# Output projection of six heads by seven half-size products, with sums of y kept in DRAM

## The chip, the cores and the metric

One core of a Trainium2 chip runs the whole step. TensorE multiplies, VectorE, ScalarE and GpSimd work on the tiles in SBUF, and DMA queues (issued by SyncE, called SP, and by GpSimd) move data to and from DRAM. The metric is the device time of one execution in microseconds. The kernel before takes 1073.28 us (median of 3 runs, 1072.37 to 1074.58).

## The reference

One step of a decoder trunk of two layers on 1024 new tokens and 8 x 4 tokens of running sequences, 1056 in all. Layer 1 is a gated linear recurrence; layer 2, where the change lies, has eight heads of 128 (HGRN2):

```python
xn = _rmsnorm(x, g_norm)
u = (xn @ w_in).astype(jnp.float32)
q, f, iv, gate = jnp.split(u, 4, axis=-1)
...                                   # per head: gated recurrence over the tokens -> o
o = o * lax.rsqrt(jnp.mean(o * o, axis=-1, keepdims=True) + EPS) * o_gain...
y = (o.reshape(Bsz, T, INNER_B) * jax.nn.silu(gate)).astype(x.dtype)
return x + y @ w_out, ...
```

The output is the RMS norm of that sum, and the new states. `y @ w_out` (1056 x 1024 by 1024 x 1024) is the output projection.

## The kernel before, in words

Activations lie transposed: a row of a head or of a model block is a tile of 128 x 1056, tokens along the free axis; NCH = 3 chunks of CH = 352, two halves of HT = 528, four quarters of QT = 264. Every float32 product is made of three fast matmuls (`mm3`, L241 to L243): operand and weight are each split into a high part (a cast, by ScalarE) and a low part (value minus high part), and high x high, low x high, high x low are added up in PSUM. "Splitting" a tile means making those two parts. `subtract(e, ...)` makes the low part by a real subtraction on engine e (L328); `low` (L312 to L315) makes it by a ScalarE copy of -x and a DMA from GpSimd's queue that adds.

Instructions are collected in a flow per engine (`pe`, `act`, `dve`, `pool`, `dma` add one each, with an estimated duration, what it reads and writes, and a priority), and a planner orders each engine's list by these before the program is built. `inherit` says whose place in memory a new tile takes. The order of each engine is fixed then; at run time the engines wait for one another by semaphores.

Layer 2's input projection of heads 1 to 7 is made in pairs of row blocks by `seven(h, a, b, order, at)`: a 2 x 2 block product by seven half-size products (the Strassen-Winograd form), each product 2 halves of 12 matmuls of 264 columns. Its order strings name the products 1 to 7; a letter b is a place where one of the four bursts of the recurrence is put between the products. burst1 to burst4 of head h hold the decay levels of head h beside the outputs of head h - 1; burst4(h) ends with `gated(h - 1)`, which writes that head's y to the row `SG[h - 1]` (two rows, by turns). In the bursts GpSimd makes `vb` (L1198) and `rst` (L1302). The decay products of a head (L1048) start in the row `Gc`, whose first one is of level 1 and 528 wide; the scalings that use them are L1039.

For heads 0 to 5 `gated` also stores y to a DRAM tensor `yd`. The output projection then has two parts. The early part takes K1 = 5 heads: 24 products of 15 matmuls (one of 8 model blocks, one of 3 chunks of 352 columns), with pieces of y read back from `yd` and split by ScalarE and then VectorE or GpSimd (`splits`, `yparts`). VectorE adds each product to x in place (L1635; `x2` lists the rows where x lies). The last six bursts (burst3 of head 7 to burst4 of "head 8", which only ends head 7) are put between its products (`SPOTS1`). The late part (`late`) takes the other three heads: 24 products of 9 matmuls, of 424, 376 and 256 columns (`OUT`), added to x by VectorE (L1732), followed by the squares, their sums and the scaling of the final norm (L1702 to L1743), which run beside it.

Of the kernel before, what the change touches and what calls it, by code (L numbers as in the profile page):

```python
# [25 lines left out]
K1 = 5  # L26
NMM = 3
HC = 1
FQ0, FQ, GV = "1267b4b35", "12b675b43", "126b74b53"
SPOTS, SPOTS0, SPOTS1 = (6, 9, 0, 2), (2, 5, -1, -1), (1, 5, 9, 13, 17, 20)  # L30
# [9 lines left out]
CH = 352  # L40
# [169 lines left out]
def tile_trunk(ctx: ExitStack, tc: tile.TileContext, xT, prm, hc, w0, wg, wo0, w1, wo1, s_in,  # L210
# [85 lines left out]
    with ExitStack() as l0:  # L296
# [603 lines left out]
        yd = [nc.dram_tensor(f"yd_{h}", (128, TOK), F32, kind="Internal").ap() for h in range(H - 2)]  # L900
# [32 lines left out]
    with ExitStack() as l1:  # L933
# [8 lines left out]
        ls2 = [fixed(f"land{i}", [128, CH], F32, p1) for i in range(1)]  # L942
# [402 lines left out]
        def burst4(h):  # L1345
            s = next(hg)
            run(together([*([gated(h - 1, *s)] if h else []), *([levels3264(h, *s), values(h, (0,))] if h < H else [])]))

# [53 lines left out]
        def seven(h, a, b, order, at=()):  # L1402
# [166 lines left out]
        yh, yl = (list(o[:4]) for o in (xh, xl))  # L1569
        flat = {k: o.rearrange("p x j t -> p (x j t)") for k, o in TB.items()}  # L1570
        for k in ((2, 0), (3, 0), (4, 0), (4, 1)):
            yh.append(flat[k][:, :TOK])
            yl.append(flat[k][:, TOK:])
        for k in range(H):
            if k < 4:
                olds = [("x", 1, k, x) for x in range(2)] + [("T", 1, i, k, x) for i in range(2) for x in range(2)]
            else:
                n, i = ((2, 0), (3, 0), (4, 0), (4, 1))[k - 4]
                olds = [("T", n, i, j, x) for j in range(4) for x in range(2)]
            for o in ("yh", "yl"):  # L1580
                for c in range(NCH):
                    inherit((o, k, c), olds)

        def splits(k, cs, eng):

            for c in cs:
                if k < H - 2:
                    x, xk = next(land)
                    dma(x, yd[k][:, chunk(c)], (("yd", k),), (xk,), 3)
                    xk = (xk,)  # L1590
                else:
                    x, xk = SG[k][:, chunk(c)], ykeys(k % 2, c * CH, CH)
# [4 lines left out]
        def yparts(c):  # L1597
            return [(yh[k][:, chunk(c)], yl[k][:, chunk(c)], (("yh", k, c), ("yl", k, c))) for k in range(K1)]

        own = []  # L1600
        for i, o in enumerate(ks):
            key = ("k", i, 1)
            inherit(key, [("s", j) for j in range(6) if j * QT < (i + 1) * CH and (j + 1) * QT > i * CH])
            own.append((o[0], key))
        own.sort(key=lambda o: max(fl.readers.get(o[1]) or [0]))
        land2 = [(o, ("land", i)) for i, o in enumerate(ls2)]
        land = chain(land2, own[:3], [(t[:, :CH], k) for t, k in rawq if k[0] == "W"], cycle(own))
        for c in range(NCH):
            for k in range(K1):
                splits(k, (c,), V if k % 3 < 2 else G)  # L1610
        splits(5, range(NCH), G)


        side = cycle(banks8[NMM:4])
        raws = cycle([r for r in rawq if r[1][0] == "raw"])
        x2 = [Gs, R[:, 3], R[:, 2], R[:, 1], Bs, B2, VT, Gc]
        old = [GK, [("W", i) for i in range(5 - NRAW)], eight("A", 0), eight("A1"), eight("B"), eight("B2"), [("VT", i) for i in range(4)],
               [("Gc", l) for l in (1, 2, 4, 8, 16, 32)]]
        last = {s: f for s, f in zip(SPOTS1, (lambda: burst3(H - 1), lambda: burst4(H - 1), lambda: burst1(H), lambda: burst2(H),
                                            lambda: burst3(H), lambda: burst4(H)))}  # L1620
        ws2 = {}
        for n, (m, c) in enumerate([(m, c) for c in range(NCH) for m in range(2)] + [(m, c) for m in range(2, KD) for c in range(NCH)]):
            if m not in ws2:
                at_ = None
                if m < 2:
                    at_ = [(flat[m + 2, 1][:, i * 640:i * 640 + 640], ("wt", m, i)) for i in range(2)]
                    for _, k in at_:
                        inherit(k, [("T", m + 2, 1, j, x) for j in range(4) for x in range(2)])
                ws2[m] = weights(wo1[m][:, :128 * K1], 128 * K1, at=at_)
                for k in ykeys(Y2 + m, 0, TOK):  # L1630
                    inherit(k, old[m])
            x, xk = x2[m][:, chunk(c)], ykeys(Y2 + m, c * CH, CH)
            dma(x, x1d[m][:, chunk(c)], (), xk, 3)
            ps, pk = product(ws2[m], yparts(c), 8 if m > 1 else 1)
            dve(CH, lambda x=x, ps=ps: V.tensor_tensor(x, ps[:, :CH], x, op=ALU.add), (pk, *xk), xk, 0)  # L1635
            if n in last:
                last[n]()
                if n == SPOTS1[1]:
                    splits(6, range(NCH), V)
                if n == SPOTS1[5]:  # L1640
                    splits(7, range(NCH), V)

# [3 lines left out]
        for m in range(KD):  # L1646
            row = (xh, xl)[m // 4][4 + m % 4]
            hi, lo, hk, lk = row[:, :nl], row[:, nl:2 * nl], ("late", m, 0), ("late", m, 1)
            for k in (hk, lk):
                inherit(k, [("x", p, m % 4, x) for p in (2, 3) for x in range(2)])  # L1650
            raw, rk = next(raws)
            dma(raw[:, :nl], wo1[m][:, 128 * K1:], (), (rk,), 1, nl / 2)
            act(nl, lambda hi=hi, raw=raw: S.copy(hi, raw[:, :nl]), (rk,), (hk,), 1)
            pool(nl, lambda hi=hi, lo=lo, raw=raw: G.tensor_tensor(lo, raw[:, :nl], hi.bitcast(F32), op=ALU.subtract), (rk, hk), (lk,), 1)
            late.append((hi, lo, (hk, lk)))
# [56 lines left out]
        for a, n in OUT:  # L1712
# [4 lines left out]
            for m in range(KD):  # L1717
# [12 lines left out]
                pe(9 * n / 2200, emit, (*wk, *((o, K1 + k, c) for o in ("xh", "xl") for k in range(K2) for c in cs)), (pk,))  # L1730
# [90 lines left out]
```

## Time and profile before

| what | value |
|---|---|
| median of 3 runs | 1073.28 us (1072.37 to 1074.58) |
| the profiled execution | 1074.84 us, its span 1073.1 us |
| mean granted TensorE clock | 0.994 |
| busy: PE, DVE, ACT, POOL | 1050.9, 745.6, 663.7, 504.5 us |
| the early part of the output projection | 942.65 to 1023.43 us |
| the late part | 1023.43 to 1061.02 us, then the tail to 1073.1 |

Times inside the profile are microseconds from the span's start. PE is TensorE's matmuls, PEld its weight loads, DVE is VectorE, ACT ScalarE, POOL GpSimd and SP the queue of DMAs. Matmuls are pipelined, so a matmul's own length is longer than its pace; the pace is read from a stretch of many.

### The profile page before, as it was taken

The page shows a single profiled execution, that of the slowest core. Times are in us where ns is not written, and L with a number is a line of the kernel's source. Part 1 is how long each engine was busy: PE and PEld are TensorE (multiplying, and loading weights), DVE is VectorE, ACT ScalarE, POOL GpSimd, SP SyncE. Part 2 cuts the span into 40 slices and gives each one's busy share as a digit, 9 for nine tenths or more (in the row PEclk, how much of TensorE's full clock was granted, in tenths as well). Part 3 has the DMA queues.
Part 4 walks back from the last instruction along what each step waited for, and adds up shares of the span by engine and source line. Part 5 has one row for each costly group of instructions (what it writes and reads, how often), then busy time and mean ns, then how long its engine had stood idle before and what let it go on. Part 6 is the DMA issues. An engine that isn't in the chain of part 4 may idle for free.

```text
span 1073.1 us, 25672 instructions
## 1 busy us (share of the span) xinstructions
PE 1050.9 (98%) x10020; PEld 1023.3 (95%) x10020; DVE 745.6 (69%) x1481; ACT 663.7 (62%) x1493; POOL 504.5 (47%) x536
## 2 busy tenths in 40 slices
PE   9999999999999999999989999999999999999997
PEld 9999999999999999999989998989999999989996
DVE  7999996887987787274887556556565475674446
ACT  6578656867765964243467685858586767652323
POOL 3425353354543547455454454455455464541544
PEclk9999999999999999999989999999999999999999
DMA  9111112124832785373675564746465657555204
GB/s 302 60 28 43 56 48 72 58 60 127 270 104 67 217 258 168 108 242 121 188 200 110 130 140 100 178 93 156 89 151 112 155 112 169 140 161 166 84 1 162
DMA packets 92490, 139.59 MB, mean 130 GB/s; under 512 B 11344, under 2 KB 60496, under 8 KB 92368
## 3 DMA queue, kind: packets, MB, share of 16 engines
q1 hardware_dynamic: 75952, 109.49, 31.8%
q0 software_dynamic: 14112, 25.70, 14.3%
q10 hardware_dynamic: 2304, 2.77, 0.8%
q8 instruction: 78, 1.28, 0.5%
q14 instruction: 44, 0.36, 0.1%
HBM read 77.54 MB, written 29.81 MB: 100 GB/s over the span
## 4 chain that ended last, share of the span: by engine, by line
PE 86%; DVE 9%; DMA 3%; issue 1%; ACT 1%; POOL 0%; POOLq 0%; ACTq 0%; SPq 0%; DVEq 0%
PE mm L241 24%; PE mm L242 24%; PE mm L243 23%; PE hg L1057 2%; PE hg L1166 2%; DMA a<-xn 1%; PE hg L1274 1%; PE hg L572 1%; DVE R L1039 1%; PE hg L1276 1%; PE hg L241 1%; PE hg L242 1%; PE hg L243 1%; PE hg L1220 1%; DVE a L1240 1%
## 5 line engine op out<-in xcount | busy, mean ns | idle before, releaser
L241 PE MATMUL mm<-xh,whi 128*128 128x352 f32 (+1 forms) x1111 | 346.6, 312 | 5.7 <-DVE sg L1510 5.7
L242 PE MATMUL mm<-xl,whi 128*128 128x352 f32 (+1 forms) x1111 | 340.7, 307 | 0.0
L243 PE MATMUL mm<-xh,wlo 128*128 128x352 f32 (+1 forms) x1111 | 340.6, 307 | 0.0
L241 PEld LDWEIGHTS mm<-xh,whi 128*128 128x128 f32 x1111 | 209.0, 188 | 8.3 <-DVE sg L1510 6.8
L242 PEld LDWEIGHTS mm<-xl,whi 128*128 128x128 f32 x1111 | 209.3, 188 | 1.5
L243 PEld LDWEIGHTS mm<-xh,wlo 128*128 128x128 f32 x1111 | 209.1, 188 | 0.0
L328 POOL TENSOR_TENSOR wlo<-wraw,whi 128x512 fp32r<-128x512 f32 (+1 forms) x72 | 96.3, 1347 | 105.7 <-ACT whi L383 97.2
L241 PE MATMUL mm<-t,whi 128*128 128x264 f32 (+1 forms) x354 | 104.0, 294 | 0.0
L243 PE MATMUL mm<-t,wlo 128*128 128x264 f32 (+1 forms) x354 | 101.8, 288 | 2.0 <-DMA wlo<-wraw 2.0
L242 PE MATMUL mm<-t,whi 128*128 128x264 f32 (+1 forms) x354 | 101.9, 288 | 0.0
L504 DVE SCALAR_TENSOR_TENSOR k<-xb,prm_sb,k 128x352 f32<-128x352 f32 (+2 forms) x144 | 90.0, 636 | 11.0 <-ACT k L501 6.3
L315 POOL DMA_DIRECT2D wlo<-wraw x59 | 51.6, 888 | 65.6 <-ACT wlo L314 46.6
L1510 DVE TENSOR_TENSOR k<-mm,k 128x264 f32<-128x264 f32 x72 | 30.7, 430 | 62.2 <-PE mm L243 59.4
L243 PEld LDWEIGHTS mm<-t,wlo 128*128 128x128 f32 x354 | 67.2, 190 | 2.3 <-DMA wlo<-wraw 2.3
L241 PEld LDWEIGHTS mm<-t,whi 128*128 128x128 f32 x354 | 67.5, 191 | 0.5 <-ACT k L1487 0.2
L242 PEld LDWEIGHTS mm<-t,whi 128*128 128x128 f32 x354 | 67.5, 191 | 0.0
L587 POOL TENSOR_TENSOR k<-X 128x352 f32<-128x352 f32 x36 | 42.8, 1198 | 47.8 <-DVE R L588 38.6
L383 ACT CAST whi<-wraw 128x512 fp32r<-128x512 f32 (+2 forms) x75 | 41.3, 569 | 31.3 <-PE mm L242 19.8
L315 POOL DMA_DIRECT2D wlo<-R x36 | 33.5, 929 | 49.7 <-ACT wlo L314 48.2
L241 PE MATMUL mm<-yh,whi 128*128 128x352 f32 x153 | 49.9, 326 | 0.0
L243 PE MATMUL mm<-yh,wlo 128*128 128x352 f32 x153 | 49.4, 323 | 0.0
L242 PE MATMUL mm<-yl,whi 128*128 128x352 f32 x153 | 49.4, 323 | 0.0
(422 smaller groups left out, 2742.1 us busy)
## 6 DMA issues: line engine op xcount, KB each, us to landing
wraw<-in_w_dram SPq DMA_DIRECT2D x88, 256.0 KB, 3.1
wlo<-wraw POOLq DMA_DIRECT2D x59, 256.0 KB, 4.1
wlo<-R POOLq DMA_DIRECT2D x36, 256.0 KB, 4.0
wraw<-in_wo_dram SPq DMA_DIRECT2D x34, 192.0 KB, 2.5
si<-in_s_in_dram SPq DMA_DIRECT2D x8, 512.0 KB, 4.5
R<-in_w_dram SPq DMA_DIRECT2D x16, 256.0 KB, 3.8
out_ss_out_dram<-si SPq DMA_DIRECT2D x8, 512.0 KB, 2.6
sg<-x1b SPq DMA_DIRECT2D x21, 176.0 KB, 3.1
```

The costliest lines, as they stand in the source:

```text
L241: T.matmul(out, wh, xh, start=first, stop=False, skip_group_check=chained)
L242: T.matmul(out, wh, xl, start=False, stop=False, skip_group_check=chained)
L243: T.matmul(out, wl, xh, start=False, stop=last, skip_group_check=chained)
L315: fl.add("POOL", 0.93, lambda: G.dma_start(dst.bitcast(F32), src, accum_op=ALU.add), (*r, *w), w, prio, n / 2)
L328: emit = lambda: e.tensor_tensor(b, x, a.bitcast(F32), op=ALU.subtract)
L383: act(m, lambda hi=hi, raw=raw, m=m: S.copy(hi[:, :m], raw[:, :m]), rk, (hk,), prio)
L504: dve(u, lambda src=src, dst=dst, sh=sh, k=k: V.scalar_tensor_tensor(dst, sh(src, k), pc("cw", 12 * k + m), dst, op0=ALU.mult, op1=ALU.add ...
L572: fl.add("PE", 0.62, lambda ps=ps, i=i, c=c: T.matmul(ps[:96, :CH], gs[:, i, :], ST[:96, chunk(c)], start=True, stop=True), (("gs",), *((" ...
L587: pool(CH, lambda x=x, a=a, b=b: G.tensor_tensor(x, a.bitcast(F32), b.bitcast(F32), op=ALU.add), (ak, bk), (xk,), 3)
L1057: T.matmul(ps[32 * j:32 * j + 32, n * w:n * w + w], B[:, o:o + 32], q(slice(o, o + 32)), start=True, stop=True, tile_position=(0, 32 * j))
L1166: T.transpose(ps[:, n * 128:(n + 1) * 128], row[:, a:a + 128], ident)
L1510: dve(QT, lambda: V.tensor_tensor(o[0], z[0], u[0], op=ALU.add), (z[1], u[1]), (o[1],), 0)
```

## The change

K1 goes from 5 to 6 heads, and the early part is made by seven half-size products as well (`seven_out`): heads 0 to 2 and 3 to 5 are the two row blocks, the token halves of 528 the two columns, and two model blocks the output's rows. Four pairs of model blocks make 4 x 7 products, each 2 halves of 9 matmuls of 264 columns. The late part keeps two heads.

The seven operands are y's blocks and four sums of them. `summed_y(h)`, called at the end of burst4, makes them with VectorE in `Gc` and in the y row as the heads come out, and stores them in the DRAM tensor `ysum` (8 places of 528 columns for each of 3 rows); heads 3 to 5 first read back what heads 0 to 2 left. `yd` is gone. `youts(p)` loads the 21 pieces and splits them: the high part by ScalarE, the low part by VectorE for row 0 and by GpSimd for rows 1 and 2 (`YSUB`). A pair's weights take four combinations by GpSimd, and for each product a cast by ScalarE and a subtraction by GpSimd (`BYDVE` is empty). The low parts of head 7's input weights, before by `low`, are now subtractions by GpSimd (products 1, 2, 6, 7) and VectorE. The bursts' places are given by the b's in `LAST`. Layer 1 and the matmuls of layer 2's input projection stay.

```diff
-K1 = 5
+K1 = 6
+BYDVE = ()
...
+LAST = "12b675b43", "126b74b53", "12b675b43", "1267543"
...
-            if h < H - 2:
-                dma(yd[h], SG[h], ykeys(h % 2, 0, TOK), (("yd", h),), 4, 528)
+        def summed_y(h):
+            if h < K1:
...
+                if h < 3:
+                    keep_y(0, SG[h][:], k1 + k2, 2)
+                    sum_y(g1, gk, y2, y1, k1 + k2, ALU.subtract)
+                    keep_y(2, g1, gk)
+                else:
+                    keep_y(3, SG[h][:], k1 + k2, 2)
+                    dma(Gc, ysum[j, :, 0:2, :].rearrange("p m n -> p (m n)"), [("ysum", n, j) for n in (0, 1)], gk, 4, 528)
+                    sum_y(g2, gk, g2, y2, gk + k2, ALU.subtract)
+                    sum_y(g1, gk, g2, g1, gk, ALU.subtract)
+                    sum_y(y2, k2, y1, g1, k1 + gk, ALU.add)
+                    keep_y(5, Gc, gk, 2)
+                    keep_y(7, y2, k2)
...
-                low(512, lo, raw, (rk,), (lk,), 2)
+                if h < H - 1:
+                    low(512, lo, raw, (rk,), (lk,), 2)
+                else:
+                    subtract(G if p in (1, 2, 6, 7) else V, 512, lo, raw, hi, (rk, hk), (lk,), 2)
...
+            for (hi, lo), j, m in pieces:
+                src, sk = ysum[j, :, place_of[p], :], ("ysum", place_of[p], j)
...
+                dma(lo.bitcast(F32), src, (sk,), (lk,), 2, 264)
+                act(HT, lambda hi=hi, lo=lo: S.copy(hi, lo.bitcast(F32)), (lk,), (hk,), 2)
+                subtract(YSUB[j], HT, lo, lo.bitcast(F32), hi, (hk, lk), (lk,), 2)
...
+        YSUB = V, G, G
...
+            def split(p):
+                (raw, rk), (hi, hk), (lo, lk) = slot[named[p]], next(his), next(los)
+                hi, lo = hi[:, :u], lo[:, :u]
+                act(u, lambda: S.copy(hi, raw), (rk,), (hk,), 2)
+                subtract(V if p in BYDVE else G, u, lo, raw, hi, (rk, hk), (lk,), 2)
...
+            combine("s", "21", "22", ALU.add)
+            combine("21", "21", "11", ALU.subtract)
+            combine("11", "11", "s", ALU.subtract)
+            combine("12", "12", "11", ALU.add)
...
+                        for j, (uh, ul, _) in enumerate(ops):
+                            w = slice(128 * j, 128 * j + 128)
+                            mm3(ps[:, :QT], (hi[:, w], lo[:, w]), uh, ul, new and j == 0, j == 2, True)
...
-            ps, pk = product(ws2[m], yparts(c), 8 if m > 1 else 1)
-            dve(CH, lambda x=x, ps=ps: V.tensor_tensor(x, ps[:, :CH], x, op=ALU.add), (pk, *xk), xk, 0)
```

GpSimd's order, from the weights of head 7 into the early part. `wlo` are low parts of weights, `xl` and `t31`, `t41` low parts of y, `wraw` and `R_73` raw weights. Before:

```order
L328 TENSOR_TENSOR wlo_128<-wraw_119,whi_124 128x512
L328 TENSOR_TENSOR wlo_129<-wraw_120,whi_125 128x128
L328 TENSOR_TENSOR xl_98<-k_85,xh_97 128x352 x2
L1302 TENSOR_TENSOR rst_5248<-rst_5248,mhalf_82 128x4
L328 TENSOR_TENSOR t30_5231<-k_85,t30_5231 128x352
L328 TENSOR_TENSOR xl_98<-k_85,xh_97 128x352
L1302 TENSOR_TENSOR rst_5248<-rst_5248,mhalf_82 128x4
L1302 TENSOR_TENSOR rst_5248<-rst_5248,mhalf_82 128x1
```

And in the changed program, from the vb of head 7's first burst:

```order
L1199 TENSOR_TENSOR vb_5250<-vst_5243,bm_92 96x512
L330 TENSOR_TENSOR xl_104<-xl_104,xh_103 128x528
L330 TENSOR_TENSOR xl_106<-xl_106,xh_105 128x528
L330 TENSOR_TENSOR t21_5230<-t21_5230,t20_5229 128x528
L330 TENSOR_TENSOR wlo_126<-wraw_119,whi_122 128x384
L330 TENSOR_TENSOR t21_5230<-t21_5230,t20_5229 128x528
L330 TENSOR_TENSOR wlo_127<-R_73,whi_123 128x384
L330 TENSOR_TENSOR t31_5232<-t31_5232,t30_5231 128x528
L1673 TENSOR_TENSOR wraw_119<-wraw_119,R_73 128x384
L330 TENSOR_TENSOR t31_5232<-t31_5232,t30_5231 128x528
L330 TENSOR_TENSOR t41_5234<-t41_5234,t40_5233 128x528
```

Where splits of 352 columns and of weights stood, rows of 528 columns and of 384 now follow one another, and the first pair's weights stand between the pieces of y.

VectorE's order between burst4 of head 5 and burst1 of head 6. `sg_148` is `Gc`, `ST_143` the gate row, `sg_145` a row of y, and `L1040` are the scalings (L1039 before). Before:

```order
L1048 TENSOR_TENSOR sg_148<-ST_143 128x528
L1510 TENSOR_TENSOR k_85<-mm_157,k_85 128x264
L1525 SCALAR_TENSOR_TENSOR R_73<-R_73,k_85 128x264
L1048 TENSOR_TENSOR sg_148<-sg_148 128x264
L1525 SCALAR_TENSOR_TENSOR R_73<-R_73,k_85 128x264
L1069 TENSOR_TENSOR R_73<-R_73,ST_143 128x1056
L1048 TENSOR_TENSOR sg_148<-sg_148 128x128
L1510 TENSOR_TENSOR k_85<-mm_156,k_85 128x264
L1048 TENSOR_TENSOR sg_148<-sg_148 128x64
L1048 TENSOR_TENSOR sg_148<-sg_148 128x32
```

And in the changed program:

```order
L1552 SCALAR_TENSOR_TENSOR R_73<-R_73,k_85 128x264
L1070 TENSOR_TENSOR R_73<-R_73,ST_143 128x1056
L1340 TENSOR_TENSOR sg_148<-sg_148 128x528
L1537 TENSOR_TENSOR k_85<-mm_156,k_85 128x264
L1340 TENSOR_TENSOR sg_145<-sg_145,sg_148 128x528
L1537 TENSOR_TENSOR k_85<-mm_157,k_85 128x264
L1552 SCALAR_TENSOR_TENSOR sg_145<-sg_145,k_85 128x264 x2
L1062 COPY_PREDICATED attnd_5236<-mask0_86,hg_162 128x256
L1062 COPY_PREDICATED attnd_5236<-mask1_87,hg_162 128x256
L1040 TENSOR_TENSOR R_73<-R_73,ST_143 128x528
L1040 TENSOR_TENSOR a_112<-a_112,ST_143 128x528
L1049 TENSOR_TENSOR sg_148<-ST_143 128x528
```

The sums (L1340; the first of three is one row above the piece) stand where the decay products stood, and the first of these, `sg_148<-ST_143`, now comes after the first scalings of burst1.

TensorE at the start of the early part. Before, the first product's matmuls (weights by `whi`, `t`), 15 of them, begin so:

```order
L241 MATMUL mm_158<-xh_93,t21_5230 128x352
L242 MATMUL mm_158<-xl_94,t21_5230 128x352
L243 MATMUL mm_158<-xh_93,t21_5230 128x352
L241 MATMUL mm_158<-xh_95,t21_5230 128x352
L242 MATMUL mm_158<-xl_96,t21_5230 128x352
```

And in the changed program, one half of the first product, 9 matmuls:

```order
L243 MATMUL mm_158<-xh_93,whi_122 128x264
L244 MATMUL mm_158<-xl_94,whi_122 128x264
L245 MATMUL mm_158<-xh_93,wlo_126 128x264
L243 MATMUL mm_158<-xh_95,whi_122 128x264
L244 MATMUL mm_158<-xl_96,whi_122 128x264
L245 MATMUL mm_158<-xh_95,wlo_126 128x264
L243 MATMUL mm_158<-xh_97,whi_122 128x264
L244 MATMUL mm_158<-xl_98,whi_122 128x264
L245 MATMUL mm_158<-xh_97,wlo_126 128x264
```

The columns fall from 352 to 264 and the heads of a product from five to three; there are 504 of these matmuls after and 360 before.

More of the change, by code (lines that the diff above doesn't have):

```diff
@@ L899, in tile_trunk @@
         masks()
-        yd = [nc.dram_tensor(f"yd_{h}", (128, TOK), F32, kind="Internal").ap() for h in range(H - 2)]
+        ysum = nc.dram_tensor("ysum", (3, 128, 8, HT), F32, kind="Internal").ap()
         x1b = [nc.dram_tensor(f"x1b_{m}", (128, TOK), F32, kind="Internal").ap() for m in range(KD)]
@@ L1606, in tile_trunk @@
[L1606 to L1611, printed above, removed]
+        x2 = [Gs, KR[:, :TOK], R[:, 2], R[:, 1], Bs, B2, VT, Gc]
+        old = [GK, [("s", i) for i in range(6)], eight("A", 0), eight("A1"), eight("B"), eight("B2"), [("VT", i) for i in range(4)],
+               [("Gc", l) for l in (1, 2, 4, 8, 16, 32)]]
@@ L1614, in tile_trunk, with then @@
+        def then(*fs):
+            return lambda: [f() for f in fs]
+        ends_ = [lambda: burst3(H - 1), then(lambda: burst4(H - 1), lambda: splits(6, range(NCH), V)), lambda: burst1(H), lambda: burst2(H),
+                 lambda: burst3(H), then(lambda: burst4(H), lambda: splits(7, range(NCH), V))]
+        for i, order in enumerate(LAST):
+            seven_out(2 * i, order, ends_[2 * i:2 * i + 2])
         side = cycle(banks8[NMM:4])
         raws = cycle([r for r in rawq if r[1][0] == "raw"])
-        x2 = [Gs, R[:, 3], R[:, 2], R[:, 1], Bs, B2, VT, Gc]
@@ L1617, in tile_trunk @@
[L1617 to L1633, printed above, removed]
-            ps, pk = product(ws2[m], yparts(c), 8 if m > 1 else 1)
-            dve(CH, lambda x=x, ps=ps: V.tensor_tensor(x, ps[:, :CH], x, op=ALU.add), (pk, *xk), xk, 0)
[L1636 to L1641, printed above, removed]
```

141 lines of the change are left out of this document (108 added, 33 removed).

## Prediction

> **What bounds the kernel now.** I read the shares and the chain of waits on the page first, then the windows of the last 130 us, since everything the change touches ends there, and last the groups of instructions and the timeline at the places where engines meet.
>
> ```profile
> PE 86%; DVE 9%; DMA 3%; issue 1%; ACT 1%; POOL 0%; POOLq 0%; ACTq 0%; SPq 0%; DVEq 0%
> 942.65:951.81 9.16, 7.16 (x32) 6.35 (x31) 6.20 (x14) 3.52 (x8) 2.69 (x4) 0.81 0.81 255
> 957.55:967.24 9.69, 9.69 (x67) 9.67 (x61) 8.71 (x16) 5.15 (x13) 6.87 (x6) 1.00 0.09 30
> 911.03:922.83 11.80, 11.80 (x98) 11.66 (x97) 7.13 (x16) 10.16 (x24) 5.97 (x7) 1.00 0.57 109
> ...
> sum 18.32, PE 18.32 PEld 16.08 DVE 8.83 ACT 7.99 POOL 4.96; mean PE 3.05 PEld 2.68 DVE 1.47 ACT 1.33 POOL 0.83
> PE mm L241 <- ACT xh L1594: 1.0, 1, 1.0
> PE mm L242 <- POOL xl L328: 0.7, 1, 0.7
> ```
>
> A window's row gives start and end, its length, the busy time of PE, PEld, DVE, ACT and POOL with instruction counts, the granted clock, the DMA share and GB/s. The line that begins with "sum" is that of the six windows that hold burst3 and burst4 of head 7 and the four bursts after them (18.32 us, PE without a gap). The two waits are those of PE in 942 to 952.
>
> TensorE is the bound: 86% of the chain. So a count of its matmuls is the first half of the sum, and what keeps it waiting the second. The first group of the output projection (which starts at 942.65, when head 7's last input product ends) is the one place near the change where PE waits today: 30 matmuls of 352 columns take 9.16 us. At the pace of the next window (60 such products' matmuls in 9.69 us, 0.1615 us each) they would take 4.85, so 4.3 us are lost, to y tiles that come back from DRAM and are then split by ScalarE, GpSimd and VectorE.
>
> **Matmuls of the early part.** Products of 264 columns run at 0.1229 us a matmul (96 in 11.80 us, the window from 911.03). Now: 24 products of 15 matmuls of 352 columns, 360 x 0.1615 = 58.1 us. With the bursts, 58.1 + 18.3 = 76.5, and with the 4.3 lost that is the 80.8 us from 942.65 to 1023.43, where the late part begins. After: 4 pairs of output rows x 7 products x 2 halves x 9 matmuls = 504 of 264 columns, 504 x 0.1229 = 61.9 us; with the same bursts 80.3. So without any stall the early part would last 0.5 us less than now, and it would carry six heads, not five.
>
> **Matmuls of the late part.** It falls from three heads to two: in each of its three column widths 8 products go from 9 matmuls to 6, 24 matmuls fewer of 424, of 376 and of 256 columns.
>
> ```profile
> 1023.43:1037.20 13.77, 13.77 (x73) 13.50 (x73) 4.72 (x8) 3.91 (x7) 5.61 (x6) 1.00 0.01 2
> 1037.20:1041.88 4.68, 4.68 (x29) 4.68 (x29) 1.70 (x3) 1.59 (x3) 2.21 (x3) 1.00 0.01 2
> 1041.88:1051.25 9.37, 9.37 (x57) 9.01 (x56) 6.12 (x17) 3.16 (x6) 5.84 (x6) 1.00 0.14 50
> 1051.25:1054.44 3.19, 3.19 (x28) 3.19 (x28) 3.19 (x7) 2.38 (x6) 2.01 (x2) 1.00 0.66 240
> 1051.25:1061.02 9.77, 9.77 (x81) 9.52 (x81) 7.41 (x19) 5.07 (x12) 5.72 (x7) 1.00 0.40 144
> ```
>
> The rows give 13.77/72 = 0.191, 4.68/27 = 0.173 and 3.19/27 = 0.118 us. 24 x (0.191 + 0.173 + 0.118) = 11.6 us less. It doesn't all stay. From 1041.88 to 1061.02 VectorE is busy 6.12 + 7.41 = 13.5 of 19.1 us: it adds each product to x and scales the finished columns, and none of that goes. PE loses there all of 24 x 0.118 = 2.8 and some 15 of the 24 matmuls of 376, 2.6: 19.1 - 5.4 = 13.7 us of PE work beside 13.5 of VectorE. Two engines level with each other wait for one another now and then. I give back 1.0 us (bounds 0 and 3, the latter if the adds queue behind the scalings at every product): -10.6. The tail after 1061 is as now.
>
> **Heads 1 to 6.** Per head one VectorE subtraction (heads 0 to 2) or three operations (heads 3 to 5) of 528 columns: 12, by the row of 528 below 0.70 us each, 8.4 us in all. VectorE is not the bound there, and the work sits behind burst4, when PE has seven's products to run. The scratch for the sums is the buffer that takes the decay products of the next head, so the first of these (L1048, at 913.44) moves behind the sums and their store, from 10 us ahead of burst1's scalings to among them, and for heads 3 to 5 a load of 528 KB lies in that chain too.
>
> ```profile
> si<-in_s_in_dram SPq DMA_DIRECT2D x8, 512.0 KB, 4.5
> 908.96 0.68 DVE L1039 TENSOR_TENSOR sg<-sg 128x512 f32<-128x512 f32 x1
> 913.44 0.71 DVE L1048 TENSOR_TENSOR sg<-ST 128x528 f32<-128x528 f32 x1 [0.32 <-ACT ST L1519]
> 924.00 0.94 DVE L1061 COPY_PREDICATED attnd<-mask,hg 128x256 f32<-128x256 uint8 x2 [2.05 <-PE hg L1057]
> ```
>
> A load of that size lands after 4.5 us. From burst4's end (908) to the scalings that burst1 releases (924) lie 16 us; 4.5 for the load, 2.1 for three sums, some 3 for the store (issue and landing) make 10. It fits, with 6 us to spare. On SP the stores of the sums wait for VectorE, and the next loads of raw weights stand behind them. I take +0.5 for six heads (0 to 3).
>
> **Where the stalls come from.** The y sums must be split into a high and a low part, as now: 21 pieces of 528 columns, 14 of them on GpSimd and 7 on VectorE, where now 18 pieces of 352 are, 6 of them on GpSimd. GpSimd also takes every subtraction and combination of the new weights (11 of 384 columns a pair).
>
> ```profile
> L328 POOL TENSOR_TENSOR wlo<-wraw,whi 128x512 fp32r<-128x512 f32 x6 | 7.7, 1290 | 19.7 <-ACT whi L383 19.7
> L1654 POOL TENSOR_TENSOR xh<-wraw,xh 128x384 fp32r<-128x384 f32 x4 | 4.0, 1008 | 3.1 <-ACT xh L1653 3.1
> L1198 POOL TENSOR_TENSOR vb<-vst,bm 96x512 fp32r<-96x512 f32 x6 | 6.2, 1036 | 12.3 <-DVE vst L1182 6.3 <-PE hg L1249 6.0
> L1302 POOL TENSOR_TENSOR rst<-rst,mhalf 128x4 f32<-128x4 f32 x6 | 6.6, 1098 | 8.1 <-DVE rst L1300 8.1
> L1305 DVE TENSOR_TENSOR kt<-hg,rst 128x512 f32<-128x512 f32 x6 | 4.1, 687 | 1.1 <-POOL rst L1302 1.1
> L1039 DVE TENSOR_TENSOR R<-R,sg 128x528 f32<-128x528 f32 x2 | 1.4, 704 | 0.0
> L1525 DVE SCALAR_TENSOR_TENSOR sg<-sg,k 128x264 f32<-128x264 f32 x8 | 3.4, 427 | 1.8 <-ACT sg L1524 1.8
> ```
>
> By the changed order, from the first vb of head 7's burst1 (about 929.3) to the last weight of the first pair GpSimd has 12 splits of 528 (1.29 x 528/512 = 1.33 each, 16.0 us), 9 operations of 384 (9.1), two vb (2.1), three rst (at most 3.3) and a small copy: about 30.5 us. The weight it ends with is wanted when the pair's seventh product starts: 942.65 + 6 products x 18 x 0.1229 (13.3) + burst3 5.74 + burst4 2.56, at 964.2. There are 34.9 us for 30.5 of work, which looks like room. But the two engines exclude each other:
>
> ```profile
> 937.75 1.47 DVE L1039 TENSOR_TENSOR R<-R,sg 128x512 f32<-128x512 f32 x1
> 939.48 0.68 DVE L1039 TENSOR_TENSOR R<-R,sg 128x512 f32<-128x512 f32 x1
> 937.39 2.14 POOL L328 TENSOR_TENSOR wlo<-wraw,whi 128x512 fp32r<-128x512 f32 x2
> 852.15 0.68 DVE L1039 TENSOR_TENSOR sg<-sg 128x512 f32<-128x512 f32 x1
> 852.75 0.68 DVE L1039 TENSOR_TENSOR R<-R,sg 128x512 f32<-128x512 f32 x1
> 852.17 2.43 POOL L1437 TENSOR_TENSOR wraw<-wraw 128x512 f32<-128x512 f32 x1
> ```
>
> A VectorE operation of 512 with both inputs in SBUF takes 0.68 us alone and 1.47 where GpSimd was at work when it began; a GpSimd operation took 2.43, not 1.29, where two such VectorE operations ran ahead of it (0.68 + 0.60 + 1.2). Each waits for the other to end. VectorE's own two-input work in the same stretch is 6 splits of 528, 8 scalings of 512, two steps of 264 and the small decay products: 6 x 0.70 + 8 x 0.68 + 2 x 0.43 + about 0.7 = 11.2 us. In turn the two need 30.5 + 11.2 = 41.7 us in 34.9: the first pair ends about 6.8 us late. That lateness is taken in parts: the bursts' scalings and evacuations stand behind GpSimd's 1.33 us splits, and PE behind them. Later pairs need 11 x 1.01 = 11.1 us of GpSimd in 15.5 us of matmuls, so they run ahead again: 1 us for the second pair's first weights, 1 for the rest. Stalls 8.8 us; bounds 0 (everything fits in GpSimd's gaps) and 16 (VectorE's blocked operations hold up the evacuations of PSUM as well, at about the 0.8 us that the row of 1.47 shows, some nine times).
>
> The Trainium skill, page "SBUF — State Buffer", section "SBUF: two separate sides", says that the port pair the two engines share is an exclusive lock, held for a whole instruction by GpSimd or by a VectorE operation with two SBUF inputs. The rows above agree, and by it VectorE's adds out of PSUM would not be held up themselves, only those queued behind a blocked one.
>
> **The sum.** Early part -0.5 (its 4.3 of stall gone, 3.8 more of matmuls) + 8.8 of new stalls; late part -10.6; heads +0.5: -1.8 us on the profiled execution's 1074.84 us (span 1073.1). That execution lies 1.6 over the median of the runs; on the median, 1073.28 - 1.8 = 1071.5.
>
> **The rivals.**
>
> (a) *The stall grows beyond the saving.* The price of the port: if VectorE's blocked operations hold up what evacuates PSUM, and the clock falls after the gaps.
>
> ```profile
> 946.60:948.60 2.00, 1.76 (x7) 1.66 (x7) 0.72 (x2) 0.00 (x0) 0.00 (x0) 0.59 0.75 209
> 948.60:950.60 2.00, 2.00 (x9) 2.00 (x9) 1.53 (x3) 0.97 (x2) 0.00 (x0) 0.55 0.93 312
> ```
>
> After the gaps around 945 the granted clock was 0.59 and 0.55 over 4 us, which costs 4 x 0.43 = 1.7 us. With 13 us of stalls in the early part in place of 8.8, two such stretches (+3.4) and +2 in the heads, the sum is -0.5 + 16.4 - 10.6 + 2 = +7.3: 1080 to 1081. It turns slower once stalls in the early part pass 10.6 us. For it: VectorE and GpSimd are each already near full in the window from 957.55 (8.71 and 6.87 of 9.69), the one that resembles most what comes. Against it: in the window from 911.03 PE ran without a gap at 5.97 and 7.13.
>
> The Trainium skill, page "TensorE: Matmul & The Clock Gate", section "What's actually happening", has the clock halved only after an idle window of about 3.4 us. By that rule gaps of 1 to 2 us with matmuls between them would leave the clock alone; the two rows show less than full clock after gaps of 1.0 and 0.7 us in the records, so the measurement speaks against relying on it.
>
> (b) *The port costs little.* GpSimd does its 30.5 us in the 34.9 there are, since splits may start as early as their loads land. Stalls of 3 us in place of 8.8, a clock that never falls: -7.6, 1065.7. For it: the loads of the first pieces are issued during head 7, and order 12, 6, 7, 5 gives the weights time. Against it: the ledger counts only work, and any wait for a load or a ScalarE cast comes on top.
>
> (c) *The late part doesn't shrink*: VectorE and the shared port set its pace, and only 6 of the 11.6 us come off; with the stalls as forecast, +2.8, 1076.
>
> **Chances and range.** My case (stalls 6 to 11) 0.40, (b) 0.24, (a) 0.26, (c) 0.10. About 0.2%, 2.1 us, is what the runs of this kernel, which spread over 2.2 us, can tell from no change. My case lies on that bound and gives 0.20 to faster, 0.16 to the same, 0.04 to slower; (b) is faster; (a) is slower, with 0.01 that it comes out level; (c) is slower but for 0.02. That makes faster 0.44, same 0.19, slower 0.37. The range reaches from a little below (b), 1063, to (a), 1081; my case alone would be 1069 to 1075.
>
> **What would show it.** The late part should begin where the early one ends, and take about 27 us from its first 424-column matmul to the last 256-column one, where it takes 37.6 now; a figure over 30 is (c). From the first matmul of 264 columns by y to the first of 424 the early part should take some 89 us: under 84 is (b), over 92 is (a). GpSimd's splits of 528 should average over 1.5 us, and PE's waits there name POOL or VectorE evacuations. Stalls of a few us in every one of heads 2 to 7, with VectorE's decay products behind the load of ysum, would make the term for the heads wrong. A granted clock at full through the first pair would take away part of (a).

## The result and the profile after

The changed kernel takes 1079.74 us (median of 6 runs, 1078.1 to 1085.34) beside 1072.73 us of the kernel before (6 runs, 1072.06 to 1074.58). The ratio is 1.007, with a 95% interval of 1.0047 to 1.0094: slower by 0.7%, where 1071.5 was forecast. Run once more on another chip (under "again" below) the ratio was 1.0045 (1.002 to 1.0069).

The profiled execution took 1078.1 us (span 1076.3), the fastest of the six, so its profile shows 3.2 us of a loss whose median is 7. Line numbers after the change are one to some thirty higher than before: the scalings are L1040, the decay products L1049, the splits L330.

From the page of the changed kernel, the chain; then its windows (columns as in the prediction) of the end of head 7's input products (936.05), burst3 of head 7 with the product ahead of it, the matmuls behind that burst, and two stretches of the late part:

```profile
PE 80%; DVE 13%; DMA 3%; issue 2%; ACT 1%; POOL 1%; POOLq 0%; ACTq 0%; SPq 0%; DVEq 0%
```

```profile
936.05:947.38 11.33, 6.56 (x53) 6.14 (x50) 10.85 (x18) 4.07 (x10) 7.50 (x7) 1.00 0.33 108
951.81:961.25 9.44, 6.43 (x165) 5.39 (x163) 9.26 (x21) 5.37 (x22) 7.26 (x7) 0.84 0.44 139
961.25:965.10 3.85, 3.85 (x25) 3.85 (x18) 1.81 (x6) 1.97 (x6) 2.77 (x4) 0.50 0.58 199
1035.20:1044.44 9.24, 9.24 (x50) 9.03 (x49) 4.62 (x8) 3.61 (x7) 5.12 (x5) 1.00 0.01 2
1052.25:1064.15 11.90, 10.33 (x71) 9.34 (x71) 10.33 (x26) 6.96 (x15) 7.05 (x8) 1.00 0.41 148
```

TensorE's share of the chain fell from 86% to 80%, VectorE's rose from 9% to 13%. In the first window TensorE works 6.56 of 11.33 us while VectorE is busy for 10.85. TensorE's waits from 800 on (us in total, times, longest) say what it stood for:

```profile
PE hg L1250 <- DVE si L1257: 3.0, 1, 3.0
PE mm L243 <- ACT os L1245: 2.5, 1, 2.5
PE mm L243 <- DVE sg L1537: 2.2, 2, 1.8
PE mm L243 <- issue: 2.2, 1, 2.2
PE hg L1788 <- DVE sg L1782: 1.6, 2, 1.1
```

The copy `os` of ScalarE (L1245) had itself waited 7.7 us for VectorE. So 2.5 of the 4.8 us without a matmul in the first window stand behind VectorE; the 2.2 us marked "issue" have no releaser in the profile (see the end). What VectorE did, and GpSimd beside it, stands in the timeline; first around 879, in the bursts between head 7's input products, then around 935:

```profile
878.43 0.42 DVE L1537 TENSOR_TENSOR sg<-mm,k 128x264 f32<-128x264 f32 x1
878.77 3.29 DVE L1040 TENSOR_TENSOR sg<-sg 128x512 f32<-128x512 f32 x1
881.99 0.42 DVE L1537 TENSOR_TENSOR sg<-mm,k 128x264 f32<-128x264 f32 x1
...
878.00 1.04 POOL L1199 TENSOR_TENSOR vb<-vst,bm 96x512 fp32r<-96x512 f32 x1
879.00 1.28 POOL L1464 TENSOR_TENSOR R<-R,wraw 128x512 f32<-128x512 f32 x1
880.25 1.26 POOL L330 TENSOR_TENSOR wlo<-wraw,whi 128x512 fp32r<-128x512 f32 x1
881.46 0.65 POOL L1051 COPY gp<-sg 128x8 f32<-128x8 f32 x1
```

```profile
923.76 0.70 DVE L330 TENSOR_TENSOR xl<-xl,xh 128x528 fp32r<-128x528 f32 x1
...
932.35 5.34 DVE L330 TENSOR_TENSOR xl<-xl,xh 128x528 fp32r<-128x528 f32 x1
937.62 2.51 DVE L1049 TENSOR_TENSOR sg<-sg 128x264 f32<-128x264 f32 x1
...
931.82 1.51 POOL L1199 TENSOR_TENSOR vb<-vst,bm 96x512 fp32r<-96x512 f32 x1
933.29 2.57 POOL L330 TENSOR_TENSOR xl<-xl,xh 128x528 fp32r<-128x528 f32 x2
935.83 1.29 POOL L330 TENSOR_TENSOR t<-t,t 128x528 fp32r<-128x528 f32 x1
937.10 1.45 POOL L330 TENSOR_TENSOR wlo<-wraw,whi 128x384 fp32r<-128x384 f32 x1
```

A VectorE split that takes 0.70 us by itself (923.76) takes 5.34. It comes up at 932.35 and is served at about 937, after `vb` and three GpSimd operations that each followed right behind the one before. At none of the three boundaries between them did VectorE get its turn, though it had been waiting. It got it at the fourth, in the midst of GpSimd's run: the subtraction at 937.10 took 1.45 us where others of its width take 1.0. What let VectorE in there is not shown. At 878.77 the same happens to a scaling of 0.68 us: 3.29. There GpSimd's run is `vb`, a combination of head 7's weights (L1464) and one of the subtractions (L330) that the change put in the place of the adding DMAs, and the evacuation at 881.99 stands behind it, for which TensorE waits 1.8 us.

Over the stages, from the profiles (us; the first 615 are the same work in all):

| stage | before | after | again | low7 (below) |
|---|---|---|---|---|
| up to burst4 of head 1 | 615.2 | 615.1 | 619.1 | 621.1 |
| to burst4 of head 5 | 233.5 | 229.1 | 230.2 | 227.7 |
| to burst4 of head 6 | 56.8 | 61.8 | 60.2 | 57.4 |
| to burst4 of head 7 | 61.8 | 63.6 | 62.4 | 58.2 |
| to the first matmul of the late part | 56.2 | 65.6 | 65.2 | 65.1 |
| late part, to its last product | 37.6 | 28.9 | 28.9 | 28.9 |

The first row differs by 4 to 6 us between executions, with the same work in it, so single spans aren't compared; the rows below it are. They show where time went, not the size of the loss: together they make +3.1 us after and +1.0 in "again", beside 7.0 and 6.0 in the medians. The kernel before has one profile only, of an execution 1.6 us over its median. Two rows need care. The stretch to burst4 of head 5 is shorter after the change: 227.7 to 230.8 us in all 16 profiles with the change in it, 233.5 before, where TensorE waited 4.9 us for VectorE's evacuations (1.6 after). No run explains that. And the stretch to burst4 of head 6 isn't steady: late_places, narrow_loads, narrow_v, split_y_vvv and narrow_g (all below), with VectorE and GpSimd in the same order there as in the changed kernel, took 56.9 to 59.0 us and had no wait of TensorE for VectorE's evacuation, which cost 1.8 us after and 1.6 in "again".

### The profile page after: what moved, and what is told of

It reads as the page before. It is cut to its first block, busy times and chain, and to the rows that moved or that the text cites. A ratio compares the mean times of both kernels' runs of the same rounds, so it can differ in the third digit from the quotient of the medians.

```text
span 1076.3 us, 25929 instructions
## 1 busy us (share of the span) xinstructions
PE 1045.6 (97%) x10092; PEld 1016.2 (94%) x10092; DVE 788.9 (73%) x1526; ACT 667.1 (62%) x1494; POOL 543.9 (51%) x566
## 3 DMA queue, kind: packets, MB, share of 16 engines
q8 instruction: 79, 1.29, 0.5%
## 4 chain that ended last, share of the span: by engine, by line
PE 80%; DVE 13%; DMA 3%; issue 2%; ACT 1%; POOL 1%; POOLq 0%; ACTq 0%; SPq 0%; DVEq 0%
PE mm L243 22%; PE mm L244 22%; PE mm L245 22%; PE hg L1058 2%; PE hg L574 1%; DVE xl L330 1%; DVE R L1040 1%; DVE t L330 1%; PE hg L1275 1%; PE hg L1167 1%; PE hg L1221 1%; PE hg L243 1%; PE hg L244 1%; PE hg L245 1%; PE hg L1277 1%
## 5 line engine op out<-in xcount | busy, mean ns | idle before, releaser
L243 PE MATMUL mm<-xh,whi 128*128 128x352 f32 (+1 forms) x1147 | 355.2, 310 | 10.5 <-DVE sg L1537 4.1
L244 PE MATMUL mm<-xl,whi 128*128 128x352 f32 (+1 forms) x1147 | 349.3, 305 | 0.0
L245 PE MATMUL mm<-xh,wlo 128*128 128x352 f32 (+1 forms) x1147 | 349.1, 304 | 0.0
L243 PEld LDWEIGHTS mm<-xh,whi 128*128 128x128 f32 x1147 | 216.3, 189 | 11.8 <-DVE sg L1537 5.0
L330 POOL TENSOR_TENSOR wlo<-wraw,whi 128x512 fp32r<-128x512 f32 (+1 forms) x83 | 112.5, 1363 | 98.5 <-ACT whi L385 75.4
L243 PE MATMUL mm<-t,whi 128*128 128x264 f32 x408 | 119.3, 292 | 1.1 <-ACT k L1514 0.6
L245 PE MATMUL mm<-t,wlo 128*128 128x264 f32 x408 | 116.6, 286 | 2.1 <-DMA wlo<-wraw 2.1
L244 PE MATMUL mm<-t,whi 128*128 128x264 f32 x408 | 116.5, 286 | 0.0
L245 PEld LDWEIGHTS mm<-t,wlo 128*128 128x128 f32 x408 | 77.4, 190 | 2.5 <-DMA wlo<-wraw 2.5
L243 PEld LDWEIGHTS mm<-t,whi 128*128 128x128 f32 x408 | 77.7, 190 | 2.1 <-ACT k L1514 0.8
L244 PEld LDWEIGHTS mm<-t,whi 128*128 128x128 f32 x408 | 77.8, 191 | 0.1
L385 ACT CAST whi<-wraw 128x512 fp32r<-128x512 f32 (+1 forms) x63 | 36.3, 591 | 20.1 <-DMA wraw<-in_w_dram 11.3
```

Of the source, the lines that this page charges most:

```text
L243: T.matmul(out, wh, xh, start=first, stop=False, skip_group_check=chained)
L244: T.matmul(out, wh, xl, start=False, stop=False, skip_group_check=chained)
L245: T.matmul(out, wl, xh, start=False, stop=last, skip_group_check=chained)
L330: emit = lambda: e.tensor_tensor(b, x, a.bitcast(F32), op=ALU.subtract)
L385: act(m, lambda hi=hi, raw=raw, m=m: S.copy(hi[:, :m], raw[:, :m]), rk, (hk,), prio)
```

## Experiments

Theory A: GpSimd's two-input operations keep VectorE's out, and VectorE's queue, with the evacuations in it, keeps TensorE waiting. Its rivals: the pieces of y come late (B), GpSimd or VectorE simply has too much work (C, D). Ratios are to the kernel before on the same chip; in one batch all share its runs, and a ratio's interval stands in brackets.

**again.** The changed kernel, unaltered.

> The changed kernel once more, for its spread and a second profile. It measured 1079.7 us (1078.1 to 1085.3) against 1072.7, and its first profile 1076.3 us of span against 1073.1. If the loss is a fixed queue (order of work), the stages repeat within 1 us: input products of head 7 about 4.4 us late, early part 87.8, late part 29.0. If it depends on which engine happens to get a shared resource first, the stages vary by several us from run to run while the order of instructions is the same.

1079.19 us, 1.0045 (1.002 to 1.0069). VectorE's split took 5.34 us again, at the same place (5.33 and 5.34 in late_places and narrow_loads too); from burst4 of head 1 on, no stage differs by more than 1.6 us. So this stall is a matter of the order, not of chance; the one near 879 came in these two profiles and not in the five named above.

**narrow_g** and **narrow_v.** The low parts of y by one engine cut to 8 columns (GpSimd's in the diff; narrow_v has `is V` in its place):

```diff
-                subtract(YSUB[j], HT, lo, lo.bitcast(F32), hi, (hk, lk), (lk,), 2)
+                e, w = YSUB[j], (8 if YSUB[j] is G else HT)
+                (pool if e is G else lambda n, f, r, w, prio: dve(n, f, r, w, prio, True))(
+                    HT, lambda e=e, w=w, lo=lo, hi=hi: e.tensor_tensor(lo[:, :w], lo[:, :w].bitcast(F32), hi[:, :w].bitcast(F32), op=ALU.subtract),
+                    (hk, lk), (lk,), 2)
```

> The 14 low parts of y that GpSimd makes are cut to 8 of 528 columns; order and waits stay, so this part of the result is left out. Theory A (GpSimd's two-input work holds off VectorE's, and VectorE's queue holds off TensorE): the stalls at burst2 of head 7 and in burst3 go, the time falls by 7 to 10 us, to 1070 to 1073. Theory B (the y pieces come late from DRAM and ScalarE's casts): those still come, the time stays within 1.5 us of 1079.7. Theory C (GpSimd only has too much work, and VectorE isn't held off): a fall of 2 to 4 us.

> The 7 low parts of y that VectorE makes are cut to 8 of 528 columns; order and waits stay, so this part of the result is left out. Theory A (held off by GpSimd): the seven narrow operations still wait for GpSimd's, as do the decay products and scalings behind them, so only 7 x 0.6 us of work goes: 1076 to 1078. Theory D (VectorE itself has too much work in front of the evacuations): 7 operations that take up to 5.3 us each are gone, and with them 6 to 9 us: 1071 to 1074. Theory B: no change.

narrow_g: 1072.0 us, 0.9986 (0.9963 to 1.001), 7.2 us under "again". narrow_v: 1076.08, 1.0021 (0.9999 to 1.0043). Both lie where A put them, and narrow_g's fall is more than C allowed. Plainest is a row of narrow_v's timeline, with GpSimd's beside it, and a later row of the same width:

```profile
931.26 4.79 DVE L1626 TENSOR_TENSOR xl<-xl,xh 128x8 fp32r<-128x8 f32 x1
941.60 0.17 DVE L1626 TENSOR_TENSOR t<-t,t 128x8 fp32r<-128x8 f32 x1 [0.21 <-ACT t L1623]
...
930.73 1.51 POOL L1199 TENSOR_TENSOR vb<-vst,bm 96x512 fp32r<-96x512 f32 x1
932.20 2.57 POOL L1626 TENSOR_TENSOR xl<-xl,xh 128x528 fp32r<-128x528 f32 x2
934.73 1.30 POOL L1626 TENSOR_TENSOR t<-t,t 128x528 fp32r<-128x528 f32 x1
```

An operation of 8 columns took 4.79 us, another one 0.17. Some 4.6 us of the first are waiting, until GpSimd's fourth operation was over.

**late_places.** `RM, SM = 3, 6` becomes `4, 7`.

> In the late part the sum of squares and the spread of the norm's factor stand after 4 and 7 products of the next width where they stand after 3 and 6. The late part takes 29.0 us where 27 were forecast. Theory E (at two thirds of the matmuls a product, three products no longer cover GpSimd's adding of the squares and VectorE's factor, TensorE waits at these places): 1.5 to 2.5 us less. Theory F (VectorE's adds and scalings set the pace of the last part): within 0.5 us, or slower, since the scaling starts later.

1079.06 us, 1.0052 (1.0026 to 1.0077): no change, theory F's side. The late part went from 28.9 to 28.1 in its profile and the tail from about 12 to 13.7.

**low7.** One part undone: head 7's weights go back to the adding DMA.

```diff
-                if h < H - 1:
-                    low(512, lo, raw, (rk,), (lk,), 2)
-                else:
-                    subtract(G if p in (1, 2, 6, 7) else V, 512, lo, raw, hi, (rk, hk), (lk,), 2)
+                low(512, lo, raw, (rk,), (lk,), 2)
```

> The low parts of head 7's input weights go back to the ScalarE copy and the adding DMA of the kernel before; the rest of the change stays. Theory A2 (a run of GpSimd operations one right behind the other keeps VectorE's two-input operation out for the whole run: 3.3 us for one of 0.7 at 878 in the first profile, 5.3 at 932): four operations of 512 on GpSimd and three on VectorE leave the stretch from 865 to 940, TensorE's stalls near 870 and 882 go, 2 to 4 us less than the change: 1075 to 1077.5. Theory H (the stalls there come from the loads and stores of the sums on the DMA queues): the adding DMAs make it no better, 1079 to 1081.

> The version with head 7's low parts by the adding DMA again, for a tighter interval beside the kernel before. If its 0.2% is real: a ratio of 0.996 to 0.999 once more, 1070 to 1073 us; if it was chance, the ratio lies around 1.000.

1072.07 us, 0.998 (0.9965 to 0.9995), and again with more runs 1072.0, 0.9978 (0.9957 to 0.9999): the whole loss is gone, more than expected, and this version beats both kernels, the one before by 0.2%, which the second interval only just tells from nothing. Windows from burst4 of head 6 to that of head 7, first low7, then the changed kernel:

```profile
906.20:964.40 58.20, 54.99 (x777) 52.85 (x776) 47.28 (x87) 42.99 (x106) 44.50 (x39) 0.97 0.79 235
```

```profile
906.00:969.60 63.60, 55.82 (x777) 53.31 (x776) 57.49 (x88) 40.65 (x102) 44.65 (x36) 0.95 0.59 194
```

GpSimd is busy for the same 44.5 us in both, TensorE does the same 777 instructions; VectorE is busy 10 us longer in the changed kernel, for one instruction more. Three low parts of weights are 2.1 us of that; the rest is mostly waiting inside instructions, as in the three splits `xl`, 8.8 us there and 3.3 in low7. The split that took 5.34 us takes 1.03 in low7: it waits for one GpSimd operation, which a small copy follows, and then a wait of GpSimd for ScalarE's cast:

```profile
934.02 1.03 DVE L330 TENSOR_TENSOR xl<-xl,xh 128x528 fp32r<-128x528 f32 x1 [2.07 <-ACT xh L1620]
...
933.49 1.00 POOL L330 TENSOR_TENSOR wlo<-wraw,whi 128x384 fp32r<-128x384 f32 x1
934.45 0.66 POOL L1051 COPY gp<-sg 128x8 f32<-128x8 f32 x1
935.45 1.32 POOL L330 TENSOR_TENSOR xl<-xl,xh 128x528 fp32r<-128x528 f32 x1 [0.34 <-ACT xh L1620]
```

**split_y_vvv** (`YSUB = V, V, V`) and **low7_vvv** (that with low7).

> All 21 low parts of y are made by VectorE (0.70 us each) and none by GpSimd (1.33 us). Theory A2: GpSimd's runs get shorter by 14 operations, 18.6 us, VectorE's own work grows by 9.8; the stalls fall nearly as when the 14 were cut to 8 columns (1072.0), 1072 to 1075. Theory D (VectorE has too much in front of the evacuations, whoever makes it wait): 9.8 us more on VectorE's queue, 1080 to 1084.

> Both edits: head 7's weights by the adding DMA, and all low parts of y by VectorE. Theory A2: the two gains come from two stretches and add up: 5 to 9 us less than the change, 1070 to 1074.5, level with the kernel before or faster by up to 0.3%. Theory H or D: 1079 or more.

1076.09 us, 1.0028 (1.0009 to 1.0047), and 1076.14, 1.002 (1.0001 to 1.0038). Neither came as expected by A2 or by D. Alone it gains 3 us, where A2 had 5 to 8 and D a loss; on low7 it costs 4. The 21 splits now stand in VectorE's own queue, ahead of what TensorE waits for, which is D's mechanism, read from these rows and not tested by itself (split_y_vvv's waits):

```profile
PE hg L1058 <- DVE sg L1040: 3.4, 1, 3.4
PE mm L243 <- DVE attns L1065: 3.1, 1, 3.1
```

**narrow_loads.** The loads of y's pieces cut to 8 columns: `dma(lo[:, :8].bitcast(F32), src[:, :8], ...)`.

> The 21 loads of y's pieces carry 8 of their 528 columns (the pieces' other columns are left out of the result); everything else stays. In all five profiles of the changed kernel or its variants TensorE stands still for 2.1 to 2.2 us at one place, the first product after burst2 of head 7, with no releaser in the profile, while the DMA engines are busy at 98% or more. Theory G (something that TensorE needs, its instructions by their own queue, waits behind the full DMA engines): that gap goes, and with the earlier pieces 2 to 4 us less, 1075.5 to 1077.5. Theory A2 alone: the gap stays, and the time is 1078 to 1080.

1079.7 us, 1.0069 (1.0041 to 1.0097): no gain. The gap without a releaser is gone, and the wait behind it grew by as much, from 2.5 to 4.8 us:

```profile
PE mm L243 <- ACT os L1245: 4.8, 1, 4.8
```

VectorE's split took 5.34 us as before, and VectorE's held queue set the time at that place whatever came before. With narrow_g, where loads and ScalarE's casts stayed and the loss went, this rules out B.

**narrow_w7_gpsimd, narrow_w7_vector, narrow_w7_both, low7_gpsimd_only.** Three cuts of head 7's subtractions in unchanged order (as in narrow_g, by engine or all, from 512 to 8 columns), and the adding DMA for GpSimd's four alone.

> Of the low parts of head 7's weights, the GpSimd ones (products 1, 2, 6, 7 of each pair) are cut to 8 of 512 columns, and that part of the result is left out; order and waits are those of the changed kernel. Theory A2 (GpSimd's time on the shared port, in runs): nearly all that the adding DMA brought, 1072 to 1074.5. Theory I (the adding DMA helped since it moved the planner's order of the early part, where burst2 and burst3 fall): the order is unchanged here, so 1077.5 to 1080.

> The counterpart: the VectorE ones (products 5, 4, 3) are cut to 8 of 512 columns, that part of the result is left out, order and waits stay. Theory A2: GpSimd's runs stay, three narrow operations per pair still wait for them; 1077 to 1079.5. Theory D (VectorE's own load): 1073 to 1076.

> All seven low parts a pair of head 7's weights (four on GpSimd, three on VectorE) are cut to 8 of 512 columns, that part of the result is left out; every engine's order and the waits are those of the changed kernel. Alone the two cuts brought 2.5 to 3 and 1.5 to 2 us. Theory A2 in full (the port time of these operations is the whole loss): 1071 to 1073, as with the adding DMA. Theory J (the adding DMA brought more since in its plan GpSimd's rows of y and weights do not stand in one long run at burst2 of head 7, where in the changed order VectorE's split waited 5.3 and, in the cut of the GpSimd ones, 8.6 us): about 1074.5 to 1076.

> Only the GpSimd ones go back to the adding DMA, VectorE keeps products 5, 4 and 3. Theory A2: between the two, nearer to the full undo: 1071 to 1074.5. Theory D: 1075.5 to 1078.

1076.69 us, 1.0023 (0.9994 to 1.0051); 1077.74, 1.0026 (1.0002 to 1.005); 1075.99, 1.0011 (0.9997 to 1.0025); and 1076.1, 1.0013 (0.9992 to 1.0034). A2's ranges held only for narrow_w7_vector; narrow_w7_gpsimd lies between A2 and I, narrow_w7_both where J put it, and low7_gpsimd_only in D's range. The cuts bring 3 to 4 us together, low7 some 7. From burst4 of head 5 to burst4 of head 7, with the same matmuls in all, the changed kernel took 125.4 us (122.6 in "again"), narrow_w7_both 120.3 and low7 115.6. Where the missing part may lie shows in narrow_w7_gpsimd, at the split of 932:

```profile
932.97 8.56 DVE L330 TENSOR_TENSOR xl<-xl,xh 128x528 fp32r<-128x528 f32 x1
...
932.44 1.51 POOL L1199 TENSOR_TENSOR vb<-vst,bm 96x512 fp32r<-96x512 f32 x1
933.91 2.59 POOL L330 TENSOR_TENSOR xl<-xl,xh 128x528 fp32r<-128x528 f32 x2
936.47 1.29 POOL L330 TENSOR_TENSOR t<-t,t 128x528 fp32r<-128x528 f32 x1
937.73 0.99 POOL L330 TENSOR_TENSOR wlo<-wraw,whi 128x384 fp32r<-128x384 f32 x1
938.69 1.29 POOL L330 TENSOR_TENSOR t<-t,t 128x528 fp32r<-128x528 f32 x1
939.94 1.02 POOL L330 TENSOR_TENSOR wlo<-R,whi 128x384 fp32r<-128x384 f32 x1
```

VectorE is passed over at all six boundaries and let in at about 941, when GpSimd's run ends at 940.96. The row of 8.5 us is there in narrow_w7_both too, and no VectorE operation above 2.3 us is in low7 from 855 to 1030. So taking away work brought about half; that low7's remaining gain is due to its other order, in which the runs fall elsewhere, is read from these rows and not shown: no run changed the order alone.

**handshake** and **low7_handshake.** A GpSimd copy of 8 columns of VectorE's low part, ahead of GpSimd's first one of each operand:

```diff
+                if j == 1:
+                    first = youtput[p][0][1]
+                    pool(8, lambda first=first: G.tensor_copy(hs, first[:, :8].bitcast(F32)), (("yo", p, 1, 0),), (("hs",),), 2)
```

> The changed kernel, and ahead of the first of GpSimd's two low parts of each y operand a GpSimd copy of 8 columns that reads VectorE's low part of the same operand: GpSimd so waits seven times for VectorE, nothing is taken away. Theory J or A2 (GpSimd's unbroken runs keep VectorE out): the longest VectorE split falls from 5.3 us to under 2.5, TensorE's wait for ScalarE's copy behind burst2 (2.6 us) goes or shrinks, 1075 to 1078 in all. If runs are not what matters (only the sum of port time): 1079.5 to 1083, for the waits come on top.

> The adding DMA for head 7's weights and the seven handshakes. In that version the longest VectorE split is 1.5 us already, so by theory J nothing more is to be had: 1071.5 to 1074. By the sum of port time alone: 1073 to 1076.

1077.79 us, 1.0045 (1.0021 to 1.0069): the time lies in J's range, but the ratio is that of "again", no gain; and 1075.72, 1.0011 (0.9995 to 1.0028), worse than low7 and in the range that the sum of port time gave, not in J's. The split went through in 1.84 us, but the run formed elsewhere and held the next operation, a scaling for which TensorE waited 5.6 us:

```profile
929.30 1.84 DVE L330 TENSOR_TENSOR xl<-xl,xh 128x528 fp32r<-128x528 f32 x1
931.05 4.20 DVE L1040 TENSOR_TENSOR R<-R,sg 128x528 f32<-128x528 f32 x1
```

```profile
PE hg L1058 <- DVE sg L1040: 5.6, 1, 5.6
```

As a cure it failed. The two times don't decide between runs and a sum of port time; the rows speak for runs, since one VectorE operation went through and the next was held for 3.5 us.

## Why the prediction was wrong, step by step

- **Early part:** near the forecast. TensorE runs 264 columns at 0.123 us in the stretches without a wait, and the stage from head 7's last input product (947.38) to the late part (1035.20) took 87.8 us, where 89 were forecast and 80.8 stood before. That is 7.5 us over the 80.3 of matmuls and bursts: TensorE stands idle for 4.3, and the rest goes with the clock (0.96 on average, 0.50 from 961.25 to 965.10), which the forecast's 8.8 of stalls did not hold.
- **Late part:** mis-sized. It fell by 8.7 us, not 10.6. The give-back is 2.9 us where 1.0 was taken, just inside the upper bound that was named (3). TensorE stands idle for 2.1 us there, and in the last stretch it and VectorE are each busy for 10.33 of 11.90 us. Moving the places where TensorE waits for the norm didn't help; which wait costs the rest stays open.
- **Heads 1 to 6:** +0.5 was forecast for everything ahead of the early part. Head 7's last input product ended at 942.65 before and at 947.38 after, 4.7 us later: +5.0 to burst4 of head 6, +4.2 from there to that product, and -4.4 up to burst4 of head 5, which nobody forecast and no run explains. This is the step that failed: the sum had no term for head 7's weights. The prediction counted GpSimd's work from 929.3 on, in the early part, and left out that the low parts of 14 weights of head 7 turn from an issue of 0.9 us on GpSimd (the DMA does the adding) into operations with two inputs, 8 on GpSimd and 6 on VectorE, from 873 to 926. To undo only this took the ratio from 1.0045 and 1.007 to 0.998, some 7 us, the whole loss. Half of that, 3 to 4 us, is shown with the order unchanged (narrow_w7_both); that the rest is the order is argued.
- **Stalls at burst2 of head 7:** the place was seen ("the bursts' scalings and evacuations stand behind GpSimd's splits") but put inside the early part's sum. TensorE stood 4.8 us there, between 936.05 and 947.38, ahead of the early part, beside 0.4 in the kernel before.
- **The port:** the mechanism was right, its rule of service wrong. "Each waits for the other to end" made the two engines take turns, and a blocked VectorE operation then costs one GpSimd operation, the 0.8 us of the row of 1.47. Many rows are like that, but VectorE was also passed over at two, three, three and six boundaries between GpSimd operations, for rows of 3.3, 5.3, 4.8 and 8.6 us. One of the prediction's own rows showed it the other way round: the GpSimd operation of 2.43 us stood behind two VectorE operations, one right behind the other. What decides when the waiting engine is let in, no run shows.
- **Rival (a)** named this side, and 1080 to 1081 us beside the 1079.74 measured, with a chance of 0.26. The clock did fall after a wait of 3.0 us. But its place was wrong: the early part stayed under the 92 us that were to show it, and more of the loss came ahead of it than (a) had put there (4.7 us in the profile, for 2). That its time fits is in part luck.
- Of the Trainium skill's pages, "SBUF — State Buffer" (section "SBUF: two separate sides") calls the port pair an exclusive lock for a whole instruction. The runs agree and go further: at up to six boundaries between two instructions the lock didn't change hands. "TensorE: Matmul & The Clock Gate" (section "What's actually happening") ties the halved clock to an idle window of about 3.4 us. Here the clock stayed at 1.00 in the window of 936.05, with gaps of 2.2 and 2.5 us and a product between them, and fell to 0.50 after the one of 3.0, which is shorter than that window.

## What to carry to other kernels

Moving a subtraction to GpSimd can cost far more than its duration when it makes a run of such operations longer: look for VectorE operations with two SBUF inputs that come up beside such a run, and for what stands behind them in VectorE's queue. An adding DMA in the place of a GpSimd subtraction leaves GpSimd 0.9 us of issue in place of 1.3 of a two-input operation; here, where a new stage already filled GpSimd, keeping the old work on the DMA was worth some 7 us. When summing a ledger, start it where the first changed instruction stands, not where the new stage begins.

## What was not expected of the hardware

- A VectorE operation of 8 columns took 4.79 us, and one of 528 took 8.56 in place of 0.70, while GpSimd ran one two-input operation after another; of these, the first took 1.51 us and the others 0.99 to 1.3, as when alone.
- In both profiles of the changed kernel and in those of three variants (late_places, narrow_v, narrow_w7_both) TensorE stood 2.1 to 2.2 us at the first product after burst2 of head 7 with no releaser in the profile, while the loads of y had kept the DMA engines at 98% up to 936. With these loads cut to 8 columns the gap was gone. That TensorE waited for its own instructions (the profile lists a queue of kind "instruction", 79 packets and 1.29 MB) fits this but wasn't shown.
- The first 615 us, the same work everywhere, took between 613.7 and 622.5 us in the profiles of the changed kernel and its variants, so a single span says little about a change of a few us.
